# A weighted copy of 33 MB into 67 MB: all loads and stores of x and out in one DMA queue, the weights alone in the other

## The chip, the cores and the metric

The kernel runs on one core of a Trainium2 chip. The metric is the device time of one execution in microseconds; lower is better. A kernel is timed several times and the median counts.

A core has engines that compute (VectorE, called DVE in the profile; ScalarE, called ACT; TensorE, called PE; GpSimd, called POOL) and an engine that only waits and issues, SyncE (SP). Data moves between HBM and the on-chip memory by DMA transfers. In this kernel SyncE and ScalarE issue them, each into a queue of its own, and the same 16 DMA engines serve both queues. In the profile, q1 is the queue that SyncE issues into and q10 is the one that ScalarE issues into. An engine carries out its instructions in program order: while it waits on a semaphore for one, those behind it wait as well.

## What is computed

```python
def reference(x, expert_indices, expert_weights):
    batch, seq, hidden = x.shape            # 16, 1024, 512
    k = expert_indices.shape[-1]            # 2
    x_expanded = x[:, :, np.newaxis, :].repeat(k, axis=2)
    weights = expert_weights[..., np.newaxis]
    return (x_expanded * weights).astype(np.float32)
```

There are 16,384 tokens with 512 float32 values each, 33.55 MB. Each token is multiplied by two weights, so that the output has two rows per token, 67.11 MB. The indices are not used.

## The kernel before, in words

The tokens are cut into 8 groups of 2,048 (`groups`, line 30). In a group each of the 128 partitions holds 16 consecutive tokens. So a load of a group brings 16 × 512 × 4 bytes = 32 KB to each partition as one contiguous row, 4 MB in all. The products of a group are 64 KB per partition, 8 MB in all.

The on-chip buffer of a group is a slot of 64 KB per partition (`slots`, line 39); there are three. A load (`load`, lines 112 to 120) writes its 32 KB into the upper half of a slot. The products then overwrite the slot from below, in place. `products` (line 133) makes both products of a run of tokens with one DVE instruction, and `ranges` cuts the 16 tokens into runs so that no run overwrites tokens that a later one still reads: 8, 4, 2 and 1 tokens (output widths 8192, 4096, 2048 and 1024 in the profile). The last token is left to ScalarE, with one multiplication for each weight (`last`, line 153).

A group is stored in two halves of 4 MB, each 32 KB per partition. The first half (line 174) is issued after the first DVE instruction of the group and the second half (line 178) after the ScalarE multiplications. Below, S3a and S3b are the halves of group 3, L3 is its load, and W the load of the weights.

The weights come once, 128 KB into 128 partitions (`weights_in`, line 66). TensorE transposes them twice and DVE copies them out (`weights_spread`, line 76), so that each partition has the 256 weights of its tokens in `w_tile` before the first product.

The schedule is written out by hand (`manual_schedule`, line 104): each engine's instructions stand in the order of the Python program, and semaphore waits are put in for the data. The program order is W, L0, L1, L2, the spreading of the weights, and then for each group i: four runs of products with S*i*a after the first, the two ScalarE multiplications, S*i*b, and, from group 1 on, load(i + 2). That load needs the slot of group i − 1, so it waits until both stores of group i − 1 have landed. L3 so stands behind S1b in the program and waits for S0a and S0b; L7, the last, stands behind S5b and waits for S4b.

Before the change SyncE issues W (line 68) and the 16 stores into q1, and ScalarE issues the 8 loads (line 120) into q10.

Of the kernel before, what the change touches and what calls it, by code (L numbers as in the profile page):

```python
# [1 line left out]

# [4 lines left out]


@with_exitstack
def kernel(  # L10
    ctx: ExitStack,
    tc: tile.TileContext,
    x: bass.AP,
    expert_indices: bass.AP,
    expert_weights: bass.AP,
    out: bass.AP,
):
    nc = tc.nc

    batch, seq, hidden = x.shape  # L20
    k = expert_weights.shape[-1]
    P = nc.NUM_PARTITIONS
    ntok = batch * seq
    assert ntok % P == 0

    f32 = mybir.dt.float32
    row = k * hidden


    groups = [16] * 8  # L30
    assert sum(groups) * P == ntok
    TX = max(groups)

    xf = x.rearrange("b s h -> (b s) h")
    of = out.rearrange("b s k h -> (b s) (k h)")
    wf = expert_weights.rearrange("b s k -> (b s) k")

    w_pool = ctx.enter_context(tc.tile_pool(name="w_pool", bufs=1))
    slots = ctx.enter_context(tc.tile_pool(name="slots", bufs=3))
    raw_pool = ctx.enter_context(tc.tile_pool(name="raw_pool", bufs=1))  # L40
    psum = ctx.enter_context(
        tc.tile_pool(name="psum", bufs=2, space=bass.MemoryType.PSUM)
    )

    w_tile = w_pool.tile([P, sum(groups) * k], f32)

    def rows(flat, done, T):
        return flat[done * P : (done + T) * P, :].rearrange("(p a) n -> p (a n)", a=T)

    B = 8
    M = P // B
    ident = w_pool.tile([P, P], f32)
    nc.gpsimd.memset(ident, 0.0)  # L55
    nc.gpsimd.affine_select(  # L56
        out=ident,
        in_=ident,
        compare_op=mybir.AluOpType.not_equal,
        fill=1.0,  # L60
        base=0,
        pattern=[[-1, P]],
        channel_multiplier=1,
    )

    def weights_in(head, G, T):
        raw_tile = raw_pool.tile([G * M, B * T * k], f32, name=f"raw{T}_tile")
        nc.sync.dma_start(
            out=raw_tile,
            in_=wf[head * P : (head + G * T) * P, :].rearrange(  # L70
                "(q a) n -> q (a n)", a=B * T
            ),
        )
        return raw_tile

    def weights_spread(raw_tile, head, G, T):
        n = T * k
        col_tile = raw_pool.tile([n, G * P], f32, name=f"col{T}_tile")
        cols = col_tile.rearrange("c (q r) -> c q r", r=B)
        step = 4  # L80
        for r0 in range(0, B, step):
            up_tile = psum.tile([n, step, G * M], f32)
            for r in range(step):
                nc.tensor.transpose(  # L84
                    up_tile[:, r, :],
                    raw_tile[:, (r0 + r) * n : (r0 + r + 1) * n],
                    ident[: G * M, : G * M],
                )
            nc.vector.tensor_copy(  # L89
                out=cols[:, :, r0 : r0 + step],  # L90
                in_=up_tile.rearrange("c r q -> c q r"),
            )
        down_tile = psum.tile([P, G * n], f32)
        for g in range(G):
            nc.tensor.transpose(  # L95
                down_tile[:, g * n : (g + 1) * n],
                col_tile[:, g * P : (g + 1) * P],
                ident[:n, :n],
            )
        nc.vector.tensor_copy(  # L100
            out=w_tile[:, head * k : (head + G * T) * k], in_=down_tile
        )

    ctx.enter_context(tc.manual_schedule())

    starts = [sum(groups[:i]) for i in range(len(groups))]
    loaded = []

    def load(i):
        if i >= len(groups):
            return
        T = groups[i]
        slot_tile = slots.tile([P, TX * row], f32)
        loaded.append(slot_tile)
        src = rows(xf, starts[i], T)
        at = T * (row - hidden)
        nc.scalar.dma_start(out=slot_tile[:, at : at + T * hidden], in_=src)  # L120


    def ranges(T):
        lo, out = 0, []
        while lo < T - 1:
            hi = lo + 1
            while (hi + 1) * k <= T * (k - 1) + lo and hi < T - 1:
                hi += 1
            out.append((lo, hi))
            lo = hi  # L130
        return out

    def products(slot_tile, T, lo, hi, w_at):
        m = hi - lo
        at = T * (row - hidden) + lo * hidden
        nc.vector.tensor_tensor(  # L136
            out=slot_tile[:, lo * row : hi * row].rearrange(
                "p (t k h) -> p t k h", t=m, k=k
            ),
            in0=slot_tile[:, at : at + m * hidden]  # L140
            .rearrange("p (t h) -> p t h", t=m)
            .unsqueeze(2)
            .to_broadcast([P, m, k, hidden]),
            in1=w_tile[:, w_at + lo * k : w_at + hi * k]
            .rearrange("p (t k) -> p t k", t=m)
            .unsqueeze(3)
            .to_broadcast([P, m, k, hidden]),
            op=mybir.AluOpType.mult,
        )

    def last(slot_tile, T, w_at):
        for c in range(T * k - k, T * k):
            nc.scalar.mul(  # L153
                out=slot_tile[:, c * hidden : (c + 1) * hidden],
                in_=slot_tile[:, T * row - hidden : T * row],
                mul=w_tile[:, w_at + c : w_at + c + 1],
            )

    raw_tile = weights_in(0, 8, 16)
    load(0)  # L160
    load(1)
    load(2)
    weights_spread(raw_tile, 0, 8, 16)

    for i, T in enumerate(groups):
        slot_tile = loaded[i]
        outr = rows(of, starts[i], T)
        w_at = starts[i] * k
        done = 0
        for lo, hi in ranges(T):  # L170
            products(slot_tile, T, lo, hi, w_at)
            if done == 0:
                done = hi
                nc.sync.dma_start(
                    out=outr[:, : done * row], in_=slot_tile[:, : done * row]
                )
        last(slot_tile, T, w_at)
        nc.sync.dma_start(
            out=outr[:, done * row :], in_=slot_tile[:, done * row : T * row]
        )  # L180
        if i:
            load(i + 2)

# [1 line left out]
_INS = ['x', 'expert_indices', 'expert_weights']  # L185
_OUTS = [((16, 1024, 2, 512), 'float32')]


# [23 lines left out]
```

## Time and profile before

| | |
|---|---|
| median of 3 runs | 240.37 us (240.29 to 241.27) |
| the profiled execution's own time | 240.02 us |
| its span, first to last instruction | 238.2 us |
| outside the span | 1.8 us |
| bytes read and written in HBM | 33.69 MB and 67.11 MB |
| DMA, mean over the span | 423 GB/s |
| DVE busy | 134.7 us (57%) |
| transfers of 4 MB | 8 loads, 16 stores |

How to read it: the page's second part cuts the span into 40 slices of 5.96 us. In the row of the DMA engines a 9 says that the 16 engines were busy for 90% or more of the slice, and the row below gives the rate. The windows view gives the same for stretches that one chooses: length, busy time of an engine with its number of instructions, the granted TensorE clock, the DMA engines' busy share and their rate. It counts a packet where it starts, so the ends of short stretches can be off by a packet. The timeline lists instructions with start and duration; "idle before" is the time the engine had nothing to do, with what ended it.

### The profile page before, as it was taken

To read this page: it belongs to the slowest core of one execution; us is meant where nothing else is said; L and a number is where in the kernel's file an instruction comes from. 1 tells how busy PE (TensorE), PEld (TensorE's weight loads), DVE (VectorE), ACT (ScalarE), POOL (GpSimd) and SP (SyncE) were. 2 spreads that over 40 slices of the span, in tenths; PEclk is the share of its full clock that TensorE was granted. 3 is DMA by queue.
4 is the path that set the end of the run, shared out by engine and by line. 5 is a ranking of instruction groups with operands and counts; after the bars stand their busy time and mean duration, and the time that the engine had idled before them with its cause. 6 is when DMAs were issued, how large, how long until landed. Compare 5 with 4: busy or idle time off the path is not lost.

```text
span 238.2 us, 201 instructions
## 1 busy us (share of the span) xinstructions
PE 2.9 (1%) x16; PEld 2.0 (1%) x16; DVE 134.7 (57%) x35; ACT 12.8 (5%) x17; POOL 0.7 (0%) x6
## 2 busy tenths in 40 slices
PE   0130000000000000000000000000000000000000
PEld 0120000000000000000000000000000000000000
DVE  0079999999900998009970299503994069910000
ACT  0020020020010001000020000200002000020000
POOL 1000000000000000000000000000000000000000
DMA  7999999999999999999999999999999999999996
GB/s 278 448 440 440 352 435 440 440 440 435 413 402 429 440 440 440 429 429 435 440 429 418 440 424 435 435 440 440 429 429 429 429 435 429 424 435 435 440 440 264
DMA packets 3600, 100.80 MB, mean 423 GB/s; under 512 B 400, under 2 KB 528, under 8 KB 528
## 3 DMA queue, kind: packets, MB, share of 16 engines
q1 hardware_dynamic: 2448, 67.24, 65.4%
q10 hardware_dynamic: 1152, 33.55, 33.4%
HBM read 33.69 MB, written 67.11 MB: 423 GB/s over the span
## 4 chain that ended last, share of the span: by engine, by line
DMA 56%; DVE 28%; ACT 2%; PE 1%; issue 0%; DVEq 0%
DMA out_dram<-slot_tile 32%; DVE slot_tile L136 28%; DMA slot_tile<-in_x_dram 20%; DMA raw_tile<-in_expert_weights_dram 4%; ACT slot_tile L153 2%; PE up_tile L84 1%; PE down_tile L95 0%; DVE col_tile L89 0%; DVE w_tile L100 0%; DVEq L136 0%
## 5 line engine op out<-in xcount | busy, mean ns | idle before, releaser
L136 DVE TENSOR_TENSOR slot_tile<-slot_tile,w_tile 128x8192 f32<-128x8192 f32 (+3 forms) x32 | 132.9, 4158 | 61.4 <-DMA slot_tile<-in_x_dram 60.6
L153 ACT ACTIVATE slot_tile<-slot_tile,w_tile 128x512 f32<-128x512 f32 x16 | 11.5, 721 | 184.8 <-DVE slot_tile L136 184.6
L89 DVE COPY col_tile<-up_tile 32x512 f32<-32x512 f32 x2 | 1.4, 678 | 12.1 <-PE up_tile L84 12.1
L84 PE MATMUL up_tile<-ident,raw_tile 128*32 128x128 f32 x8 | 1.9, 415 | 10.9 <-DMA raw_tile<-in_expert_weights_dram 10.9
L153 ACT ACT_TABLE_LOAD x1 | 1.3, 1283 | 13.3 <-DMA slot_tile<-in_x_dram 13.3
L84 PEld LDWEIGHTS up_tile<-ident,raw_tile 128*32 128x32 f32 x8 | 1.0, 139 | 11.3 <-issue 10.9
L100 DVE COPY w_tile<-down_tile 128x256 f32<-128x256 f32 x1 | 0.4, 425 | 1.2 <-PE down_tile L95 1.2
L95 PE MATMUL down_tile<-ident,col_tile 32*128 32x32 f32 x8 | 1.1, 292 | 0.8 <-DVE col_tile L89 0.8
L95 PEld LDWEIGHTS down_tile<-ident,col_tile 32*128 32x128 f32 x8 | 0.9, 214 | 1.3 <-DVE col_tile L89 1.3
L56 POOL TENSOR_SCALAR_AFFINE_SELECT ident<-ident 128x128 f32<-128x128 f32 x1 | 0.3, 293 | 0.1
L55 POOL MEMSET ident<- 128x128 f32 x1 | 0.2, 204 | 0.3 <-POOLq L196 0.3
L196 POOL MEMSET const-bfloat16-1.0<- 128x1 bf16 x1 | 0.1, 102 | 0.0
L196 POOL MEMSET const-uint8-127<- 128x1 uint8 x1 | 0.1, 102 | 0.0
L196 POOL MEMSET const-float32-0.0<- 128x1 f32 x1 | 0.1, 99 | 0.2 <-issue 0.2
L196 POOL MEMSET const-float32-1.0<- 128x1 f32 x1 | 0.1, 99 | 0.0
## 6 DMA issues: line engine op xcount, KB each, us to landing
out_dram<-slot_tile SPq DMA_DIRECT2D x16, 4096.0 KB, 38.0
slot_tile<-in_x_dram ACTq DMA_DIRECT2D x8, 4096.0 KB, 23.9
raw_tile<-in_expert_weights_dram SPq DMA_DIRECT2D x1, 128.0 KB, 10.0
```

Of the source, the lines that this page charges most:

```text
L55: nc.gpsimd.memset(ident, 0.0)
L56: nc.gpsimd.affine_select(out=ident, in_=ident, compare_op=mybir.AluOpType.not_equal, fill=1.0, base=0, pattern=[[-1, P]], channel_multipl ...
L84: nc.tensor.transpose(up_tile[:, r, :], raw_tile[:, (r0 + r) * n : (r0 + r + 1) * n], ident[: G * M, : G * M],)
L89: nc.vector.tensor_copy(out=cols[:, :, r0 : r0 + step], in_=up_tile.rearrange("c r q -> c q r"),)
L95: nc.tensor.transpose(down_tile[:, g * n : (g + 1) * n], col_tile[:, g * P : (g + 1) * P], ident[:n, :n],)
L100: nc.vector.tensor_copy(out=w_tile[:, head * k : (head + G * T) * k], in_=down_tile)
L136: nc.vector.tensor_tensor(out=slot_tile[:, lo * row : hi * row].rearrange("p (t k h) -> p t k h", t=m, k=k), in0=slot_tile[:, at : at + m ...
L153: nc.scalar.mul(out=slot_tile[:, c * hidden : (c + 1) * hidden], in_=slot_tile[:, T * row - hidden : T * row], mul=w_tile[:, w_at + c : w_ ...
L196: nc = _bacc.Bacc("TRN2", target_bir_lowering=False, num_devices=1)
```

## The change

The load of the weights is issued by ScalarE in place of SyncE, and the loads of x by SyncE in place of ScalarE. The order of the program, sizes, slots and arithmetic are the same. SyncE then issues L0, L1, L2, S0a, S0b, S1a, S1b, L3, S2a, S2b, L4, and so on to L7, S6a, S6b, S7a, S7b, all into q1; ScalarE issues W alone into q10.

```diff
     def weights_in(head, G, T):
         raw_tile = raw_pool.tile([G * M, B * T * k], f32, name=f"raw{T}_tile")
-        nc.sync.dma_start(
+        nc.scalar.dma_start(
             out=raw_tile,
...
         src = rows(xf, starts[i], T)
         at = T * (row - hidden)
-        nc.scalar.dma_start(out=slot_tile[:, at : at + T * hidden], in_=src)
+        nc.sync.dma_start(out=slot_tile[:, at : at + T * hidden], in_=src)
```

## The prediction

> **What bounds the kernel now.** I began with the page's slices, because a kernel that moves 100 MB and computes little is likely to hang on its transfers.
>
> ```profile
> span 238.2 us, 201 instructions
> PE 2.9 (1%) x16; PEld 2.0 (1%) x16; DVE 134.7 (57%) x35; ACT 12.8 (5%) x17; POOL 0.7 (0%) x6
> ...
> DMA  7999999999999999999999999999999999999996
> GB/s 278 448 440 440 352 435 440 440 440 435 413 402 429 440 440 440 429 429 435 440 429 418 440 424 435 435 440 440 429 429 429 429 435 429 424 435 435 440 440 264
> ...
> q1 hardware_dynamic: 2448, 67.24, 65.4%
> q10 hardware_dynamic: 1152, 33.55, 33.4%
> ```
>
> The DMA row is 9 in every slice but the first and the last, and the two queues' packets fill 65.4 + 33.4 = 98.8% of the 16 engines' span. No compute engine is near that: DVE has 57%. The rate sits near 432 GB/s throughout, with one plain hole: the fifth slice, 352. The 98.8% can be read wrongly, though: a packet that is held up counts as busy. So the rate, not the busy share, tells where time was lost.
>
> The chain of waits names DVE with 28% of the span, so I asked what DVE waits for.
>
> ```profile
> DVE slot_tile L136 <- DMA slot_tile<-in_x_dram: 60.6, 5, 12.4
> ```
>
> Five times DVE stands idle for a load, 60.6 us in all. DVE is on the chain only while it delays no transfer that the engines could have made, and the timeline of ScalarE's queue shows that it doesn't.
>
> ```profile
> 0.73 1.36 ACTq L120 DMA_DIRECT2D slot_tile<-in_x_dram  x3
> ...
> 53.12 0.33 ACTq L120 DMA_DIRECT2D slot_tile<-in_x_dram  x1
> ...
> 82.30 0.34 ACTq L120 DMA_DIRECT2D slot_tile<-in_x_dram  x1
> ...
> 111.45 0.33 ACTq L120 DMA_DIRECT2D slot_tile<-in_x_dram  x1
> ...
> 140.53 0.34 ACTq L120 DMA_DIRECT2D slot_tile<-in_x_dram  x1
> ...
> 169.51 0.34 ACTq L120 DMA_DIRECT2D slot_tile<-in_x_dram  x1
> ```
>
> Each of the five late loads is issued when the second half of an earlier store has landed. They stand 29.18, 29.15, 29.08 and 28.98 us apart. Per group 3 × 4.19 MB must move, so a 4 MB transfer takes 29.1 / 3 = 9.7 us, which is 432 GB/s. That is the whole period: the engines are the bound, group by group. The windows view, cut at these issues, says where this does not hold.
>
> ```profile
> core 0: us, DVE busy (x), PEclk, DMA share, GB/s
> 0.00:1.70 1.70, 0.00 (x0) 1.00 0.00 0
> 1.70:4.10 2.40, 0.00 (x0) 1.00 1.18 395
> 4.10:12.80 8.70, 0.68 (x1) 1.00 1.02 437
> 12.80:24.00 11.20, 9.97 (x4) 1.00 1.00 430
> 24.00:30.00 6.00, 5.97 (x2) 1.00 0.94 350
> 30.00:53.10 23.10, 22.96 (x7) 1.00 1.00 431
> 53.10:82.30 29.20, 16.75 (x5) 1.00 1.00 431
> ...
> 169.50:236.90 67.40, 28.18 (x8) 1.00 0.99 428
> ```
>
> The loss outside the ends is in 24 to 30: 6.0 × (432 − 350) / 432 = 1.14 us. This is where the first store enters beside running loads (SyncE issues it at 23.82, below). Everything from 30 on runs at 428 to 431, with loads and stores mixed or with stores alone.
>
> **The change part by part.** Removed: nothing. Added: nothing. The bytes, the 24 transfers and the weights stay, so the floor stays: 24 × 9.7 = 232.8 us of transfers, beside 1.7 us before the first packet. What changes is the order in which the engines meet the transfers. Now two queues share them; afterwards one queue hands them over in program order.
>
> *Does the one queue ever run empty?* I follow it. By 24.0 the rows above have moved 2.4 × 395 + 8.7 × 437 + 11.2 × 430 = 9,570 KB of the 12,710 KB of W, L0, L1 and L2; the rest takes 7.3 us, and with the packet in flight L2 is through at about 32. From there each transfer takes 9.7 us (ends, rounded): S0 51.5, S1 71, L3 80.5, S2 100, L4 109.5, S3 129, L5 138.5, S4 158, L6 167.5, S5 187, L7 197, S6 216, S7 235.5. Against that stand the times at which each transfer can be issued. Of groups 0 to 2 they are those of now, since DVE works on loads that come no later:
>
> ```profile
> 0.74 0.38 SPq L68 DMA_DIRECT2D raw_tile<-in_expert_weights_dram  x1
> ...
> 15.10 50.03 DVE L136 TENSOR_TENSOR slot_tile<-slot_tile,w_tile 128x8192 f32<-128x8192 f32 x12
> 23.82 0.34 SPq L174 DMA_DIRECT2D out_dram<-slot_tile  x1
> ...
> 33.37 0.33 SPq L178 DMA_DIRECT2D out_dram<-slot_tile  x1
> ...
> 40.47 0.33 SPq L174 DMA_DIRECT2D out_dram<-slot_tile  x1
> ...
> 50.02 0.33 SPq L178 DMA_DIRECT2D out_dram<-slot_tile  x1
> ...
> 57.11 0.33 SPq L174 DMA_DIRECT2D out_dram<-slot_tile  x1
> ...
> 66.67 0.33 SPq L178 DMA_DIRECT2D out_dram<-slot_tile  x1
> ```
>
> S0a is ready at 23.8 and its turn comes at 32; S0b 33.4 for 42; S1a 40.5 for 51.5; S1b 50.0 for 61. The tightest spare time is 8 us. Later groups, from a load's end, need one run of 8.7 us for the first half and all of DVE and ScalarE for the second:
>
> ```profile
> L136 DVE TENSOR_TENSOR slot_tile<-slot_tile,w_tile 128x8192 f32<-128x8192 f32 x8 | 69.5, 8689 | 60.6 <-DMA slot_tile<-in_x_dram 60.6
> ```
>
> ```profile
> 192.67 16.74 DVE L136 TENSOR_TENSOR slot_tile<-slot_tile,w_tile 128x8192 f32<-128x8192 f32 x4 [11.52 <-DMA slot_tile<-in_x_dram]
> ...
> 209.44 1.48 ACT L153 ACTIVATE slot_tile<-slot_tile,w_tile 128x512 f32<-128x512 f32 x2 [26.79 <-DVE slot_tile L136]
> ```
>
> That is 9 and 18.5 us with the hand-overs. S3a is ready at 89.5 for 109.5; at the end, S7a at 206 for 216 and S7b at 215.5 for 226. So the queue always holds something.
>
> *The new waits.* SyncE now waits inside its order: L3 for S0b's landing, and S2a is queued behind L3. S0b lands at 51.5, so L3 leaves at about 52 and S2a, ready at 57.1, is not delayed. L4 waits for S1b (71), and S3a behind it is ready at 89.5; L5 for S2b (100), with S4a behind it ready at 118.5; the last, L7, for S4b (158), with S6a ready at 176.5. Each load leaves 19 us or more before its turn. The eight issues cost SyncE 0.33 to 0.45 us each, in time in which it waits now for DVE. ScalarE is rid of its waits and issues; nothing on the path waits for it. The price of all this is nothing while the 8 us of queue hold; if they were gone, each microsecond by which a store is late would be one of the time.
>
> *W on the other queue.* Both issues at the start leave at 0.73 and 0.74, from either engine, and the two queues swap roles. W must reach `w_tile` before the first product, now at 15.1. S0a has 8 us to spare, so W could be that much later without effect. I take nothing.
>
> *The stall at 24 to 30.* The queues' packets, MB and shares in these 6 us:
>
> ```profile
> q10 hardware_dynamic: 48, 1.57, 74.0%
> q1 hardware_dynamic: 16, 0.52, 20.2%
> ```
>
> In the new order the first store follows L2 in the same queue and enters beside nothing. Bounds: −1.14 us (the stall belongs to two queues meeting) and 0 (it belongs to the first store of the program, and comes again at 32). It is nearer to the first: the same first store is at work from 30 on at 431, and the loss falls where loads are still three quarters of the bytes. I take −1.14.
>
> *The changes of direction.* In q1 loads turn to stores six times and stores to loads five times. No stretch of now has this in one queue. The nearest row is around 183, where the store queue pauses between two transfers, so that loads run alone and stores come back:
>
> ```profile
> 180.00:182.50 2.50, 1.15 (x1) 1.00 1.03 446
> 182.50:185.00 2.50, 0.00 (x0) 1.00 0.97 419
> 185.00:187.50 2.50, 0.00 (x0) 1.00 0.97 419
> ```
>
> ```profile
> q10 hardware_dynamic: 32, 1.05, 101.1%
> q1 hardware_dynamic: 16, 0.00, 0.4%
> ```
>
> The second fence has the queues in 182.6 to 185 (packets, MB, share): only loads moved bytes. The mean of the three rows is 428, so the going and coming cost 7.5 × 4 / 432 = 0.07 us. The farther rows are the start, 2.4 × (432 − 395) / 432 = 0.21 us for the first load packets, and 1.14 us for the stall. Bounds per change: 0 to 1.14 us. I take 0.07 for each of six pairs, 0.4 us.
>
> *The sum.* 240.02 − 1.14 + 0.4 = 239.28 for a profiled execution. The median of the runs lies 0.35 above the profiled one, so 239.6, or 0.3% less than 240.37. A measurement of this kernel can tell about 0.5%, 1.2 us, from no change; my forecast lies inside.
>
> **Rivals.** *All losses go (238.7).* Loads alone ran at 437 in 4.1 to 12.8, against 432 mixed. If L3 to L7 run so, 5 × 9.7 × 5 / 437 = 0.55 us go, and with free changes of direction another 0.4. For it speaks the row of 437; against it 430 in 12.8 to 24, loads alone too.
>
> *Nothing changes (240.4 to 240.8).* The first store's stall moves to 32, and the changes of direction cost 0.4 or nothing. For it: the stall comes only once, with the first store. Beside this stands a rule of the Trainium skill, "DMA: Bandwidth & Descriptors", section "Issuing engines are not separate DMA queues": transfers from any issuing engine run on the same 16 engines, and a second issuer saves only issue time. By that rule the time would be that of now; the trace agrees in that both queues together hold 432 GB/s, with the 350 as its exception.
>
> *Slower: a change of direction in one queue empties the engines (241.5 and up).* Place: the 11 changes from L2/S0a to L7/S6a. Mechanism: now an engine fills the start of a load with a store of the other queue; with one queue nothing stands beside it. Price: at the 0.21 of the first load packets 11 × 0.21 = 2.3, so 240.37 − 1.14 + 2.3 = 241.5; at 1.14 it would be 251.8. It decides over the gain from 1.14 / 11 = 0.10 us per change, and is slower by over 0.5% from about 0.21. Against it: in the mixed stretches the engines serve both queues side by side at 431, and neighbouring transfers of one kind follow without a gap (169.5 to 236.9, stores but for one load: 428). A rule of the Trainium skill speaks for it: "SBUF — State Buffer", section "The DMA setup-cost knee", gives every transfer about 2 us that do not scale with its bytes, mostly the confirmation of the last byte. If 11 changes laid that bare it would be an estimated 22 us; the trace shows none of it between neighbours of one kind, and no row shows a neighbour of the other kind in the same queue.
>
> *SyncE's order holds a store back (over 241.6).* It needs a load to leave later than the store behind it is ready, 5 us at the nearest place (L3 and S2a), and then the queue's 23 us of work to be used up. I give it 0.02.
>
> **How the numbers follow.** The forecast has a chance of 0.44, with 0.10 of it below 239.17 (faster by over 0.5%) and 0.34 inside, since the stall and the small terms scatter by some tenths. All losses go: 0.20. Nothing changes: 0.14. Direction: 0.20, and its mild half lies below 242.6. SyncE's order: 0.02. Faster is 0.10 + 0.20 = 0.30, the same 0.34 + 0.14 = 0.48, slower 0.20 + 0.02 = 0.22. The range reaches to just beyond the first rival and takes in the milder half of the third, up to 0.3 us per change of direction (240.37 − 1.14 + 11 × 0.3 = 242.5): 238.6 to 242.6. It leaves out some 0.12 above and a few hundredths below.
>
> **What would show it.** Right: no fifth slice below 400, and rates near 432 at each change of direction; all rows of SyncE's queue with L3 issued near 52 and S1b, S2a not later than now; DVE waiting for loads as before or longer, at no price. The last landing comes 1 us earlier. Wrong: a dip again at the first store, now near 32 (the second rival); eleven dips, one per turn, with the period per group over 29.1 us (the third); slices with DMA below 9 and SyncE waiting with an empty queue behind it (the fourth).

## The result and the profile after

| | before | after |
|---|---|---|
| median | 240.19 us (22 runs, 239.35 to 241.27) | 241.20 us (22 runs, 240.05 to 243.26) |
| ratio | | 1.005, 95% interval 1.003 to 1.007 |
| profiled execution | 240.02 us | 240.61 us |
| its span | 238.2 us | 238.8 us |

The change made the kernel slower by 0.5%, where a gain of 0.3% was forecast. Besides the median, the scatter grew: seven of the 22 runs after lie above 242, none of before does. The profiled execution after, at 240.61, is below that median, so its trace shows less than the typical loss.

The page of the kernel after, slices and queues:

```profile
span 238.8 us, 199 instructions
...
DMA  7999999999999999999999999999999999999994
GB/s 269 453 442 439 439 351 439 434 434 423 434 406 439 434 428 434 439 439 439 439 439 428 439 423 423 439 423 434 417 439 439 428 439 439 428 439 434 434 434 214
...
q1 hardware_dynamic: 3456, 100.66, 98.4%
q10 hardware_dynamic: 144, 0.13, 0.2%
```

All the 4 MB transfers now go through q1, and the DMA row is 9 in every slice but the first and the last: the one queue never ran empty. But the hole is still there. It was the fifth slice (352) and is now the sixth (351). The windows view of the kernel after, cut where the turn (the change of direction in the queue) from L2 to S0a lies, and below it q1 in 28 to 32:

```profile
core 0: us, PE busy (x) PEld busy (x) DVE busy (x) ACT busy (x) POOL busy (x), PEclk, DMA share, GB/s
28.00:34.00 6.00, 0.00 (x0) 0.00 (x0) 5.93 (x3) 0.00 (x0) 0.00 (x0) 1.00 1.02 371
34.00:53.10 19.10, 0.00 (x0) 0.00 (x0) 19.00 (x6) 2.89 (x4) 0.00 (x0) 1.00 1.00 432
53.10:82.30 29.20, 0.00 (x0) 0.00 (x0) 14.76 (x5) 1.44 (x2) 0.00 (x0) 1.00 1.00 432
82.30:236.90 154.60, 0.00 (x0) 0.00 (x0) 82.97 (x20) 7.21 (x10) 0.00 (x0) 1.00 1.00 430
```

```profile
q1 hardware_dynamic: 48, 1.57, 114.6%
```

The last numbers of a window row are the DMA share and the rate. The rate dips to 371 while the share is 1.02: the engines are "busy" with packets that take longer. The queue row gives their length: 48 packets filled 114.6% of 16 engines × 4 us = 73.3 us, so 1.53 us each. They are the last three load packets of each engine, and the very last ones are the slowest. Before, the store packets in 24 to 30 took 20.2% of 96 us for 16, 1.21 us each. This is how a stall inside a transfer shows: share at or above 1, rate down.

SyncE's queue kept the predicted timetable:

```profile
52.66 0.33 SPq L178 DMA_DIRECT2D out_dram<-slot_tile  x1
53.10 0.66 SPq L120 DMA_DIRECT2D slot_tile<-in_x_dram  x1
59.75 0.33 SPq L174 DMA_DIRECT2D out_dram<-slot_tile  x1
69.30 0.33 SPq L178 DMA_DIRECT2D out_dram<-slot_tile  x1
72.82 0.34 SPq L120 DMA_DIRECT2D slot_tile<-in_x_dram  x1
```

L3 left at 53.1 (52 was forecast), L4 at 72.8 (71), and S2a behind L3 was issued as soon as its products were done, 2.6 us later than before. What did drift is the landing of the loads. DVE starts on a group when its load has landed on all 16 engines, so DVE's timeline is a clock for the slowest engine:

```profile
82.10 16.74 DVE L136 TENSOR_TENSOR slot_tile<-slot_tile,w_tile 128x8192 f32<-128x8192 f32 x4 [14.33 <-DMA slot_tile<-in_x_dram]
111.29 16.73 DVE L136 TENSOR_TENSOR slot_tile<-slot_tile,w_tile 128x8192 f32<-128x8192 f32 x4 [12.45 <-DMA slot_tile<-in_x_dram]
140.42 16.74 DVE L136 TENSOR_TENSOR slot_tile<-slot_tile,w_tile 128x8192 f32<-128x8192 f32 x4 [12.40 <-DMA slot_tile<-in_x_dram]
169.67 16.74 DVE L136 TENSOR_TENSOR slot_tile<-slot_tile,w_tile 128x8192 f32<-128x8192 f32 x4 [12.51 <-DMA slot_tile<-in_x_dram]
199.30 16.73 DVE L136 TENSOR_TENSOR slot_tile<-slot_tile,w_tile 128x8192 f32<-128x8192 f32 x4 [12.89 <-DMA slot_tile<-in_x_dram]
```

The steps are 29.19, 29.13, 29.25 and 29.63, against 29.1 for three transfers. The last two lose 0.15 and 0.5 us, in a stretch whose mean rate is 430.

### The profile page after: what moved, and what is told of

Its sections match the earlier page's. It is cut to its first block, busy times and chain, and to the rows that moved or that the text cites. A ratio compares the mean times of both kernels' runs of the same rounds, so it can differ in the third digit from the quotient of the medians.

```text
span 238.8 us, 199 instructions
## 1 busy us (share of the span) xinstructions
PE 2.9 (1%) x16; PEld 2.0 (1%) x16; DVE 134.7 (56%) x35; ACT 12.8 (5%) x17; POOL 0.7 (0%) x6
## 4 chain that ended last, share of the span: by engine, by line
DMA 59%; DVE 28%; ACT 2%; PE 1%; issue 0%; DVEq 0%; SPq 0%
DMA slot_tile<-in_x_dram 33%; DVE slot_tile L136 28%; DMA out_dram<-slot_tile 21%; DMA raw_tile<-in_expert_weights_dram 5%; ACT slot_tile L153 2%; PE up_tile L84 1%; PE down_tile L95 0%; DVE col_tile L89 0%; DVE w_tile L100 0%; DVEq L136 0%; SPq L120 0%
## 6 DMA issues: line engine op xcount, KB each, us to landing
raw_tile<-in_expert_weights_dram ACTq DMA_DIRECT2D x1, 128.0 KB, 12.7
```

## The experiments

Four theories stood behind the expectations. **A:** in one queue, the last packets of a load are slow on some engines when stores follow it; the engines that lag lag more at each turn, and the slowest of the 16 sets the end. **B:** the weights come later (TensorE starts on them at 13.54, it was 10.91), and so does all of DVE's work. **D:** one queue costs something per transfer, whatever the order. **E:** SyncE's order holds stores back. Apart from these, the hole at the first store asks whose it is. Each ratio is to before, run beside the kernel on the same chip; it lies near the quotient of the means, not of the medians, so single late runs count in it. A turn to stores is a place in a queue where a load is followed by a store; the kernel after has six.

**The kernel after, again**

> The changed kernel itself, for a second profile and more times. Its runs so far scatter from 240.05 to 243.26 around 241.2, those of before from 239.35 to 241.27 around 240.2. Theory A (in the one queue, each load that a store follows ends with slow packets, and the slowest of the 16 engines sets the end): the profile shows slow last packets of the loads again, and the last landing moves with their sum; an execution near 242 shows more of them than the one of 240.61. Theory B (the weights now arrive 2.6 us later and DVE runs later): nothing in the transfers after 33 us differs from before except a queue that waits for a store.

Measured: 241.11 (240.45 to 243.63), ratio 1.0068 (1.0041 to 1.0095). The loss and the scatter repeat. The profiled execution, 240.49, was again below the median. Its DVE steps are 29.24, 29.12, 29.12 and 29.55; the runs above 242 left no trace here.

**Only the weights in the other queue**

```diff
-        nc.sync.dma_start(          # weights; loads stay on nc.scalar
+        nc.scalar.dma_start(
```

> Only the weights change queue (ScalarE's); loads stay on ScalarE's queue behind them, stores on SyncE's. Theory A: as before, 240.2 within 0.3, since loads and stores are still in two queues. Theory B: with the weights ahead of the loads in one queue they land by about 3 us, DVE starts at L0's landing, and the time falls or stays; it can't show the loss.

Measured: 240.73 (240.27 to 241.27), ratio 1.0031 (1.0016 to 1.0046): 0.7 us over the 240.01 of before, which neither theory had. The weights are very early now, as TensorE's first row shows, but the loads are issued behind them:

```profile
0.73 0.37 ACTq L68 DMA_DIRECT2D raw_tile<-in_expert_weights_dram  x1
...
1.13 1.42 ACTq L120 DMA_DIRECT2D slot_tile<-in_x_dram  x3
...
2.99 1.87 PE L84 MATMUL up_tile<-ident,raw_tile 128*32 128x128 f32 x8 [2.99 <-DMA raw_tile<-in_expert_weights_dram]
```

The first load leaves at 1.13 in place of 0.73; the profiled spans differ by as much (238.6 and 238.2). This would explain 0.4 of the 0.7 us; the rest stays open. The kernel after has no such delay: its L0 leaves at 0.73.

**All transfers in SyncE's queue**

```diff
-        nc.scalar.dma_start(        # weights, against the kernel after
+        nc.sync.dma_start(
```

> Weights, loads and stores all in SyncE's queue. The weights then land near 3 us and not at 12.9. Theory A: the time of the changed kernel, 241.2 within 0.5, with the same scatter. Theory B: the loss goes, 240.2 or less.

Measured: 242.64 (239.99 to 243.62), ratio 1.0082 (1.0051 to 1.0114). Theory B falls: the weights are early again and the loss is there, with the same scatter. The median is 1.4 us over the 241.2 that theory A gave. The first load leaves at 1.17 here, again behind the weights, which would be 0.4 of it; the rest is not explained. The profiled execution here, 243.0, shows the loss at full size. Its DVE timeline:

```profile
82.99 16.74 DVE L136 TENSOR_TENSOR slot_tile<-slot_tile,w_tile 128x8192 f32<-128x8192 f32 x4 [19.21 <-DMA slot_tile<-in_x_dram]
112.86 16.74 DVE L136 TENSOR_TENSOR slot_tile<-slot_tile,w_tile 128x8192 f32<-128x8192 f32 x4 [13.14 <-DMA slot_tile<-in_x_dram]
142.50 16.73 DVE L136 TENSOR_TENSOR slot_tile<-slot_tile,w_tile 128x8192 f32<-128x8192 f32 x4 [12.90 <-DMA slot_tile<-in_x_dram]
172.14 16.74 DVE L136 TENSOR_TENSOR slot_tile<-slot_tile,w_tile 128x8192 f32<-128x8192 f32 x4 [12.90 <-DMA slot_tile<-in_x_dram]
201.70 16.73 DVE L136 TENSOR_TENSOR slot_tile<-slot_tile,w_tile 128x8192 f32<-128x8192 f32 x4 [12.82 <-DMA slot_tile<-in_x_dram]
```

Steps of 29.87, 29.64, 29.64 and 29.56: every group loses 0.5 to 0.8 us. How many engines lose it shows at the end, in the windows view and, below it, q1 after 236.6:

```profile
232.50:236.20 3.70, 0.00 (x0) 0.00 (x0) 0.00 (x0) 0.00 (x0) 0.00 (x0) 1.00 1.00 434
236.70:239.70 3.00, 0.00 (x0) 0.00 (x0) 0.00 (x0) 0.00 (x0) 0.00 (x0) 1.00 0.15 66
```

```profile
q1 hardware_dynamic: 14, 0.20, 10.4%
```

Up to 236.2 all 16 engines move data at 434. After 236.6 only 0.20 MB are left, six packets of 32 KB, with eight small ones for the semaphores. Packets that start where another ends can be strung together, and then 13 engines finish by 236.8 and three at 239.8 to 239.9, with two last data packets each. The same three strings have a slow packet among the last two of each of L4, L5 and L6, by 0.6 to 0.75 us, and in L7 by 0.3 to 0.4, while no other string lost more than 0.14 at any of these turns. That is theory A in one picture: after the first turn, where all 16 lose, 13 engines lose next to nothing, and the time is that of the other three.

The trace also tells which packet it is. In L4, L5 and L6 it is the load packet that a late engine still has under way when the others begin with the store behind it. In L5 the three slow packets start at 138.6 to 139.1 and end at 140.5 to 140.9, and the other 13 strings start their first store packet at 139.4 to 139.9. The two strings that end last in the kernel after show it too, in L7: their last load packets run from 197.1 to 198.7 or 198.8, 0.4 us too long, and the first of the other strings start S6a at 197.4. So an engine that is late is late by more after the turn.

**An early small store**

```diff
+    nc.scalar.dma_start(out=probe_tile, in_=ident[:16, :])   # scratch in HBM, 8 KB
     raw_tile = weights_in(0, 8, 16)
```

> The changed kernel with one more store, 16 rows of 512 bytes of the identity into a scratch buffer in HBM, issued by ScalarE ahead of the weights; nothing reads it. It asks whose the stall at the first store is (about 1 us, now at 29 to 33). If it belongs to the first store of an execution, whatever runs beside it: slow packets near 3 us and none near 30, time 241.2 or up to 1 us less. If it belongs to the change from a long run of loads to stores: still there at 29 to 33, time 241.2.

Measured: 244.17 (241.78 to 244.51), ratio 1.0163 (1.0131 to 1.0195), far more than the 241.2 at most that was expected. The small store held the weights back (they took 16.8 us to land), so that S0a was issued only at 31.53, when the last packets of L2 were already under way. Its first packets start at 32.4, half a microsecond after most engines had finished L2, so for that time the queue was dry:

```profile
28.00:34.00 6.00, 0.00 (x0) 0.00 (x0) 5.97 (x2) 0.00 (x0) 0.00 (x0) 1.00 1.02 437
34.00:66.00 32.00, 0.00 (x0) 0.00 (x0) 31.79 (x9) 2.89 (x4) 0.00 (x0) 1.00 0.99 426
66.00:84.00 18.00, 0.00 (x0) 0.00 (x0) 7.12 (x4) 1.44 (x2) 0.00 (x0) 1.00 1.00 386
```

No dip at the first turn, but one at 66 to 84, around S1b, L3 and S2a: 18 × (432 − 386) / 432 = 1.9 us. In the trace the last packets of S1b and the last two of L3 are slow on nearly all engines. So a turn in q1 with the next transfer already queued can cost all engines a microsecond, also from stores to loads, and it need not be the first turn of the execution. This run alone cannot say whether the early store or the dry queue took the first dip away; the next two do. Why its usual time is 2.4 us above its profiled one is not settled.

**The early store behind the weights**, small and large

```diff
     raw_tile = weights_in(0, 8, 16)
+    nc.scalar.dma_start(out=probe_tile, in_=ident[:16, :])   # or in_=fill_tile, 512 KB
```

> As e4, but the small store stands behind the weights in ScalarE's queue, so that the weights are not late and S0a is in the queue well before L2 ends. If the stall near 30 belongs to the first store of an execution, it has gone here. If it belongs to the turn from loads to stores with the store already queued, all 16 engines show slow load packets at 29 to 31 again; in e4 they were absent because the store was issued only at 31.5, when the loads were done.

> As e8, with an early store of 512 KB (128 rows of 4 KB of zeros into a scratch buffer that nothing reads) in place of 8 KB, in ScalarE's queue behind the weights, beside L1. It costs 1.2 us of transfer by itself. If the stall of about 1 us is paid once, where the first store with some weight meets loads on the engines: slow load packets near 14 to 25 and none at 29 to 32; time of the changed kernel plus some 0.2 to 1.2, 241.3 to 242.4. If it belongs to the turn L2 to S0a whatever came before: slow packets at 29 to 32 as in e8, and the time is 1.2 us over the changed kernel, 242.3.

Measured: 241.23 (240.26 to 241.88), ratio 1.0040 (1.0020 to 1.0059), with 8 KB; 242.53 (242.30 to 243.48, four runs), ratio 1.0102 (1.0071 to 1.0132), with 512 KB. The windows view of the two kernels:

```profile
28.00:34.00 6.00, 0.00 (x0) 0.00 (x0) 5.93 (x3) 0.00 (x0) 0.00 (x0) 1.00 1.00 366
```

```profile
28.00:34.00 6.00, 0.00 (x0) 0.00 (x0) 5.93 (x3) 0.00 (x0) 0.00 (x0) 1.00 1.01 377
```

The dip is there both times. An earlier store does not take it away: it belongs to the turn from L2 to S0a with S0a waiting in the queue. Both early stores moved rows shorter than 32 KB, 512 bytes and 4 KB; that the first store of 32 KB rows by itself makes the dip is spoken against by the run above, where S0a was the first one and made none.

**Fewer turns**

```diff
-        if i:
-            load(i + 2)
+        for j in {2: (3, 4, 5), 4: (6, 7)}.get(i, ()):
+            load(j)
```

> The changed kernel with the late loads bunched: L3, L4, L5 behind S2b and L6, L7 behind S4b, so that the one queue changes direction 5 times (3 times from loads to stores) and not 11 times (6). Theory A (the last load packets before a turn to stores are slow on the engines that lag, the same engines lag at every turn, and the slowest sets the end): the loss over 240.0 shrinks about with the 5 later turns to stores that become 2, from 1.1 us to some 0.4: 240.4, highest below 242.5; spread of the last landing over the engines below 1 us. Rival D (one queue costs the same whatever the order, for each transfer): 241.1. Rival E (a load that comes later in SyncE's order holds stores back): slower than 241.1, DMA below 9 somewhere, since L3 now leaves 10 us later.

Measured: 240.21 (239.86 to 242.37) with before at 240.41, ratio 1.0012 (0.9990 to 1.0034). One queue, the same 24 transfers, and no loss can be told; the interval leaves room for 0.8 us, and one of 12 runs still reached 242.37. Theories D and E fall: both asked for 241.1 or more. DVE waits 34.1 us for L3, where it was 14.3 in the kernel after, and it costs nothing. The windows view:

```profile
28.00:34.00 6.00, 0.00 (x0) 0.00 (x0) 5.93 (x3) 0.00 (x0) 0.00 (x0) 1.00 1.03 350
34.00:236.00 202.00, 0.00 (x0) 0.00 (x0) 116.47 (x29) 11.54 (x16) 0.00 (x0) 1.00 1.00 433
236.40:240.00 3.60, 0.00 (x0) 0.00 (x0) 0.00 (x0) 0.00 (x0) 0.00 (x0) 1.00 0.00 0
```

The first turn costs its dip; after it 202 us pass at 433, and no engine starts a data packet after 236.4.

**More turns, and their control**

```diff
...
+        for h in halves:                       # 16 KB rows; n is half a load's row
+            nc.sync.dma_start(
+                out=slot_tile[:, at + h * n : at + (h + 1) * n],
+                in_=src[:, h * n : (h + 1) * n],
+            )
...
+                if i:                          # many turns alone: behind S*i*a
+                    load(i + 2, (0,))
...
-            load(i + 2)
+            load(i + 2, (1,))
```

> The changed kernel with each late load in two halves of 16 KB rows, the first behind the first half of the store, the second behind the second: 21 changes of direction, 11 from loads to stores. To be read against e7, which has the same halves side by side. Theory A: more turns, more loss: 1 us or more above e7, spread of the last landing well over 1 us. Rival D: as e7 within 0.3.

> The control for e6: every load in two halves of 16 KB rows, one right behind the other, so 11 changes of direction as in the changed kernel. All theories: the changed kernel's time (241.1) plus what smaller packets cost, at most 1 us.

Measured: 243.27 (242.33 to 244.09), ratio 1.0129 (1.0100 to 1.0158), with 11 turns to stores; 240.81 (240.20 to 242.47), ratio 1.0036 (1.0012 to 1.0061), with the same halves side by side and 6 turns. Five more turns to stores cost 2.46 us by the medians, 0.5 each (2.2 us by the ratios). By the ratios, 3 turns cost 0.1%, 6 turns 0.4 to 0.7% and 11 turns 1.3%; the intervals are too wide to say whether each turn costs the same. The end of the kernel with many turns:

```profile
232.50:236.60 4.10, 0.00 (x0) 0.00 (x0) 0.00 (x0) 0.00 (x0) 0.00 (x0) 1.00 0.94 408
237.60:240.20 2.60, 0.00 (x0) 0.00 (x0) 0.00 (x0) 0.00 (x0) 0.00 (x0) 1.00 0.09 38
```

In the last 2.6 us 38 GB/s move where 16 engines move 432: one or two engines are still at work.

**Two queues, exchanged and with bunched loads**

```diff
-        nc.scalar.dma_start(out=slot_tile[:, at : at + T * hidden], in_=src)
+        nc.sync.dma_start(out=slot_tile[:, at : at + T * hidden], in_=src)
...
-                nc.sync.dma_start(          # both stores, and the weights
+                nc.scalar.dma_start(
```

The edit above is the exchange, against before. The bunched kernel is before with the edit of "Fewer turns".

> Before with the two queues exchanged: loads in SyncE's, stores and weights in ScalarE's. Loads and stores are still in two queues. Theory A: 240.3 within 0.4, no engine falls behind by more than 1 us. If what costs is that SyncE issues the loads, or that the loads start ahead of the weights: 241.1, as the changed kernel.

> Before (two queues) with the late loads bunched as in e5: L3, L4, L5 issued behind group 2 and L6, L7 behind group 4. It asks whether e5's order helps where no queue changes direction. Theory A: it has nothing to save, 240.3 within 0.4. If bunching itself is what e5 gained from: up to 0.9 below 240.4.

Measured: 240.71 (239.97 to 241.75), ratio 1.0022 (1.0001 to 1.0043), exchanged; 240.33 (239.63 to 242.26), ratio 1.0009 (0.9988 to 1.0029), before with the late loads bunched. Bunching gains nothing that can be told where loads and stores have queues of their own, so the gain of the fewer turns is a gain on turns. The exchanged kernel lies between before and after, about 0.5 us from each. Its interval reaches from nothing to 1.0 us, so by itself it leaves open how much "loads in SyncE's queue" cost. The kernel with fewer turns bears on that: its loads are in SyncE's queue as well, and at 1.0012 it shows no loss.

None of these kernels is shown to be faster than the one before.

## Why the prediction was wrong

*What bounds the kernel: right.* The transfers do, in both kernels, and no wait of a compute engine shows in the time: DVE's longest, 34.1 us with fewer turns, cost nothing.

*The queue never runs empty, the new waits: right.* The five late loads left within 2 us of the forecast, and the bunched loads leave far later still without cost.

*W on the other queue: right in its price, wrong in a detail.* The weights were taken to keep their time; they landed 2.6 us later, since the loads' packets came first on the engines. S0a was issued 2.6 us later too, at 26.46, still ahead of its turn, as the 8 us of spare time said. That there was a limit, the first early store showed.

*The stall at 24 to 30, "I take −1.14": this step failed.* The stall came again at 28 to 34. The argument was that it fell while loads were most of the bytes and that two queues met there. The trace of before tells otherwise once the stretch is cut at 27.7. The queues in 25.2 to 27.7, and below them in 27.7 to 30:

```profile
q10 hardware_dynamic: 31, 1.02, 124.2%
```

```profile
q1 hardware_dynamic: 16, 0.52, 52.7%
q10 hardware_dynamic: 1, 0.03, 5.3%
```

In the first stretch there are 31 load packets of 1.60 us in the mean, and not one store packet; in the second come the first 16 store packets, 1.21 us each. The slow packets stand ahead of the first store and not beside it, just as at the end of L2 in the kernel after. What the runs show is that the stall goes with this passage from loads to a store that is already issued: it is there with two queues (350), with one queue (371), with an earlier small or large store (366, 377), and with bunched loads (350). The row of 350 was the price of load packets with a store due behind them, and was read as the price of a second queue. Without this step the sum would have been 240.02 + 0.4 + 0.35 = 240.8, which is the rival "Nothing changes", whose place, the first store's stall moved to about 32, came true.

*The changes of direction, "0.07 for each of six pairs": mis-sized.* Six pairs were to cost 0.4 us. Measured on the time, a turn to stores costs about 0.5 us (2.46 us for five, many turns against control, on one chip), and three turns fewer than the kernel after bring 0.3 us each by the medians (241.11 and 240.21, on two chips). Two things went wrong in the working. The row at 183 was from two queues, and the runs show that the order within one queue costs what the order within two does not. And the price was a mean over 16 engines, as every rate in a windows row is. The rate after the first turn was indeed 430 to 432 in the kernel after; what ends the kernel is its last engine, and a loss that hits the same engines at each turn adds up without showing in a mean: to 3 us in the execution of 243.0.

*The rivals.* The slower one was the right one, with the right place and nearly the right bound (from 0.21 us per change it is slower by over 0.5%), but its mechanism was that a turn empties the engines. It doesn't: after the first turn, 13 of 16 lost next to nothing in the trace of 243.0.

The rule of the Trainium skill beside it, in "SBUF — State Buffer", section "The DMA setup-cost knee", is not borne out as a price of turns: 2 us at 11 changes would be an estimated 22, and the loss is 1. The rule of the Trainium skill in "DMA: Bandwidth & Descriptors", section "Issuing engines are not separate DMA queues", holds for the rate, 432 GB/s by one queue or by two; that the choice of queue saves nothing but issue time is not what was measured, for here it is 0.5% of the time.

*The range.* That 241.2 lies inside 238.6 to 242.6 says nothing for the main line: the range had been drawn out to take in the milder half of the slower rival.

*What stays open.* Why a load packet is slow when a store is due behind it or when other engines have begun with theirs, no run shows. Nor is it shown why an engine is late in the first place, and why one turn hits all engines for a microsecond and later ones a few. The runs after above 242 left no trace, so that a few late engines make these too is argued from the traces of 240.61 and of 243.0, the latter of the all-SyncE kernel. And part of the loss, up to 0.3%, may come with the weights on ScalarE's queue, as the kernels with only that or with exchanged queues suggest; the loss in the all-SyncE kernel shows that it isn't the whole.

## What to carry to other kernels

A kernel that is bound by its transfers, like this one, ends with its slowest DMA engine, so look at what is still moving in the last microseconds, and at the spread of landings, before trusting a mean rate. If loads and stores share one queue, try bunching them: here the cost went with the turns, not with the number of transfers. With a queue for each, the order within them mattered little here.

## What the runs showed of the hardware that was not expected

The last load packets in front of a queued store were slow: in the kernel after, the last three packets of L2 on each engine, 32 KB and otherwise 1.21 us each, took 1.53 us in the mean. In one execution three of 16 engines lost 0.6 to 0.75 us at each of three later turns, always the same three, on the packet that they had under way while the others began to store, and the other engines lost next to nothing. And an 8 KB store ahead of a 128 KB load in the same queue, both beside full traffic of the other queue, made the load take 16.8 us in place of 12.7.
